# The z projection moved into the q, k, v stage of a hybrid decoder step

## The chip, the cores and the metric

The kernel runs on one core of a Trainium2 chip. The metric is the device time of one execution in microseconds (us). A profile is one such execution taken by the hardware profiler; its span runs from the first to the last instruction. Engines are named as in the profile: PE (matmul), PEld (its weight load), DVE, ACT, POOL, and SP, which here only issues transfers.

## The reference, cut to what matters

One layer works on 2048 new positions of one sequence (`x_prompt`) and on 8 x 8 sample tokens (`x_sample`), all in float32:

```
u = rmsnorm(h, norm_mix) @ w_in                       # 1024 -> q 512, k 256, v 256, z 512, xbc 1024, dt 8
q, k, v, z, xbc, dt = split(u)                        # rope on q, k
att = dilated window attention over q, k, v           # windows (128,1), (512,4), (2048,16), merged by their lse
xbc = silu(conv4(xbc));  y = chunked SSD(xbc, dt)     # Mamba-2, chunks of 128 positions
ssm = rmsnorm((y + d_skip * x) * silu(z)) * ssm_norm
h = h + concat(att, ssm) @ w_out
h = h + relu(rmsnorm(h) @ w_up)**2 @ w_down           # 1024 -> 4096 -> 1024
return rmsnorm(h), new k, v, conv and ssm states
```

The gate z is first needed by `silu(z)` of the SSD branch. Only the normalised input block and w_in's z columns are needed to compute it.

## The kernel before, in words

Every float32 product is taken as three matmuls of split operands: a tile is written as hi + lo, and `mm3` adds hi x hi, hi x lo and lo x hi in one PSUM bank. A split is one ACT copy and one DVE subtraction (`split`).

**First stage: q, k, v.** The 2048 positions are 8 blocks of 256 (`NB`, `BS`); the first two also carry 32 sample positions each (288 columns). `prep_x(i)` squares a block, sums it, takes the root (`rstd`, small matmuls `ps_r`), scales and splits it into four tiles `xq` (8 buffers, so two blocks stay on chip) and stores it to the scratch tensor `xn_s[i]`. Block i's turn is `qk_part` (6 groups of 24 matmuls, `ps_qk`, one per 128 rows of q and k) and `v_part` (2 or 3 position tiles of 24 matmuls, `ps_v`). In the middle of the turn, before group 2, stands `prep_x(i + 1)`. Groups are evicted by ACT and DVE into stage tiles `st`, which every second turn go out by 26 q stores and 16 k stores of 32 to 256 KB on SP's queue; k also goes out through a tile `kf` (2 buffers, `O["kT"]`), v through `vf` and its split differences `vhl` (1 buffer, `v3_s`). All PSUM tiles of the stage come from the pool `pa`, which has three of the eight banks.

**Second stage: attention.** 16 steps (4 key heads x 4 position blocks): `att_load` and `att_a` load k, q and v rows from scratch, take scores (`ps_qk` of line 573) and their maximum; `att_b` takes exponentials, splits them, multiplies with v (`ps_pv`) and sums (`ps_den`); `att_c` closes a head.

**Beside it: the other projections.** `g2(grp)` computes four 128-row groups of the z, x, B, C part over all 8 blocks (`ps_xz`, 24 matmuls for each group and block): it loads four weight tiles and then each block's four tiles `xq` again from `xn_s`, evicts with ACT (`ev`, line 797) and stores to `xz_s`. Its tiles lie in a pool `yp` that is open from the start of the program, so that its first loads lie in the first stage, held behind `k.gate`, the load of block 3. `g2(0)` and `g2(4)` are x, B and C; each block's first matmul is held behind an attention step (`k.steps`, two behind). `g2(8)` is z: it is written behind the attention, ahead of branch 0, held behind step 14, with four further buffers for its later blocks (`y8`).

**Third stage: branch 0, then the rest.** `branch(0)` does the SSD's first four chunks of 128 positions (`ssd`: convolution on DVE in line 904, transposes `ps_xt`, `ps_bt`, products `ps_y`, `ps_st`, `ps_yo`, the gated norm with `ps_ss`) and merges the attention outputs of the first 512 positions (`am<-o_s`). Then come output projection (`ps_o`) and MLP (`ps_up`, `ps_dn`) over four blocks of 512 positions, with the other branches in their shadow. The first `ps_o` matmul is held behind the last matmul that `mm3` issued (`k.zl`).

What sets the order: the kernel is written as above, and a scheduler places each engine's instructions in one fixed order, from the order of writing, the dependences and the holds named here. At run time each engine, and SP's queue, works in that order.

Of the kernel before, what the change touches and what calls it, by code (L numbers as in the profile page):

```python
# [110 lines left out]
def build(nc, tc, ctx, I, O, dbg=None, stop=None):  # L111
# [33 lines left out]
    yp = p1x.enter_context(tc.tile_pool(name="g2", bufs=1, reuse_waits="tile", side="right"))  # L145
# [7 lines left out]
    k.gate = None  # L153
# [17 lines left out]
    def load_w(src, pool=None, rp=None, after=None):  # L171
        rp = rp or yp
        if rp is yp:
            raw = yp.tile([P, 4 * NBX], F32, tag="xq", name="raw", bufs=XQ)[:, :D].rearrange("p (k m) -> p k m", k=KT)
        else:
            raw = gp.tile([P, KT, P], F32, tag=rp, name="raw")
        behind(nc.sync.dma_start(raw, src), k.gate if rp is yp else None)
        pl, nb = (pool, 2) if pool else (wp, GW)
# [38 lines left out]
    gp = g1x.enter_context(tc.tile_pool(name="g1", bufs=1))  # L217
# [6 lines left out]
    def load_x(i):  # L224
        n = nblk(i)
        xr_t[i] = []
        for q in range(2):
# [4 lines left out]
            xr_t[i] += [xr[:, 0:2, :n], xr[:, 2:4, :n]]
        if i == XG:
            k.gate = k.x
        tq_t[i] = gp.tile([P, 2, NBX], F32, tag="tq", name="tq", bufs=2)
        behind(nc.sync.dma_start(tq_t[i][:, :, :n], I["tabq"][i, :, :, :n]), k.x)

    def prep_x(i):
# [12 lines left out]
        rs = rstd(gp, ss, n, 1.0 / D)  # L251
# [9 lines left out]

    load_x(0)
# [16 lines left out]
    stage = {}
    v_t = {}  # L280
    for i in range(NB):
# [15 lines left out]
        def qk_part():  # L297
            for m in range(6):
                if m == 2 and i + 1 < NB:
# [8 lines left out]
                if m in (0, 4):  # L308
# [65 lines left out]
        def v_part():  # L374
# [3 lines left out]
            for (o, p0, mrows, c) in tiles:  # L378
                pv = slice(p0, p0 + mrows)
                ps = pa.tile([P, 512], F32, tag="pa", name="ps_v")[:mrows, :NV]  # L380
# [16 lines left out]
                vhl = gp.tile([P, 3, NKV, 2, HD], F32R, tag="vhl", name="vhl", bufs=1)  # L397
# [102 lines left out]
    g1x.close()  # L500
    if stop == "g1":
# [274 lines left out]
    def g2(grp, y8=None):  # L776
        ws = [load_w(I["wxz"][m]) for m in range(grp, grp + GR)]
        for i in range(NB):
            n = nblk(i)
            xn = []  # L780
            for q in range(4):
                pl, nb = (y8, Y8B) if y8 and i >= Y8 and q else (yp, XQ)
                xq = pl.tile([P, 4 * NBX], F32R, tag="xq", name="xq", bufs=nb)
# [3 lines left out]
            for m in range(grp, grp + GR):  # L787
# [4 lines left out]
                if m == grp and PACE and 2 * grp + i >= FST:  # L792
                    tc.add_manual_dep(f.ins, (k.steps[ZST] if grp == 8 else k.steps[max(0, 2 * grp + i - FST)]).ins.name,
# [4 lines left out]
                dq('z8' if grp == 8 else 'xz').dma_start(xz_s[m, :, i * BS:(i + 1) * BS], ev[:, :BS])  # L798
                if i < 2:
                    dq('z8' if grp == 8 else 'xz').dma_start(xzs_s[m, :, i * DS:(i + 1) * DS], ev[:, BS:])  # L800
# [276 lines left out]
    with tc.high_priority(offset=-G2LAG):  # L1077
        g2(8, p1x.enter_context(tc.tile_pool(name="y8", bufs=1, reuse_waits="tile", side="right")))
# [601 lines left out]
```

## Time and profile before

| | |
|---|---|
| median of 3 runs | 2765.54 us (2765.01 to 2772.32) |
| the profiled execution | 2767.76 us, span 2766.0 us |
| PE busy | 2617.2 us (95%) |
| DVE, ACT, POOL busy | 1710.1, 1161.3, 483.8 us |
| DMA | 481.62 MB, mean 174 GB/s |
| from 889 us to the end (output projection, MLP) | PE busy 1864.64 of 1877 us |

A row of busy time by stretch gives the stretch, its length, and each engine's busy time with its instruction count. A wait row gives who waited for whom, the sum, how often and the longest. A timeline row gives start, duration, engine, line, operation, output<-inputs, shapes, and in brackets the idle time before it and what ended it. A busy PE is a pipelined one: the spans of matmuls overlap, so a rate is a stretch divided by its count.

### The profile page before, as it was taken

Reading aid. Unit: us, or ns where it says so; the run is one execution under the profiler, and the core shown is the slowest. Engines: PE = TensorE matmul, PEld = TensorE weight load, DVE = VectorE, ACT = ScalarE, POOL = GpSimd, SP = SyncE. Lnnn points to the kernel's source line nnn. Section 1 sums busy time; section 2 is a strip of 40 time slices with the busy share of each in tenths; the row PEclk is TensorE's granted clock in tenths of the full one; section 3 lists DMA queues with packets and bytes.
Section 4 is the critical chain, followed back from the end, with each engine's and each line's share of the span. In section 5 each row is a group of like instructions: output and inputs, shape, how many; then the busy total and the mean of one; then the engine's idle time right before and its main releaser. Section 6 shows DMA issues by size and latency. Waiting matters only on the chain.

```text
span 2766.0 us, 42046 instructions
## 1 busy us (share of the span) xinstructions
PE 2617.2 (95%) x15190; PEld 2275.0 (82%) x15190; DVE 1710.1 (62%) x2995; ACT 1161.3 (42%) x2243; POOL 483.8 (17%) x406
## 2 busy tenths in 40 slices
PE   7979699999968999999999999999999999999998
PEld 7979688999857778888888886667688889999998
DVE  5545467777975646777567874445487764554555
ACT  5434245455643423444444442233254434332333
POOL 2222233544531200111210110020010003000000
PEclk9989899999988999999999999999999999999999
DMA  6887877786865745543574545456464534533332
GB/s 226 242 242 230 224 212 232 235 257 211 249 209 150 226 130 162 159 146 126 164 235 142 161 138 170 142 189 202 141 191 145 158 103 153 170 100 106 105 100 85
DMA packets 355265, 481.62 MB, mean 174 GB/s; under 512 B 38608, under 2 KB 230288, under 8 KB 354016
## 3 DMA queue, kind: packets, MB, share of 16 engines
q1 hardware_dynamic: 328592, 455.26, 53.3%
q10 hardware_dynamic: 26464, 23.66, 2.6%
q8 instruction: 120, 1.97, 0.3%
q14 instruction: 89, 0.73, 0.1%
HBM read 383.42 MB, written 128.96 MB: 185 GB/s over the span
## 4 chain that ended last, share of the span: by engine, by line
PE 80%; DMA 10%; DVE 4%; SPq 2%; issue 2%; POOL 1%; ACT 1%; ACTq 0%; DVEq 0%; POOLq 0%
PE ps_dn L1068 9%; PE ps_dn L1070 9%; PE ps_up L1070 9%; PE ps_up L1068 9%; PE ps_dn L1071 9%; PE ps_up L1071 9%; PE ps_qk L573 3%; PE ps_xz L186 2%; PE ps_xz L189 2%; PE ps_xz L190 2%; DMA xq<-xn_s 2%; PE ps_o L1070 2%; PE ps_o L1068 2%; PE ps_o L1071 2%; DMA xr<-xb 2%
## 5 line engine op out<-in xcount | busy, mean ns | idle before, releaser
L847 ACT ACTIVATE wm_h<-raw_m 128x512 fp32r<-128x512 f32 x576 | 362.3, 630 | 844.3 <-PE ps_dn L1070 484.2
L848 DVE TENSOR_TENSOR wm_l<-raw_m,wm_h 128x512 fp32r<-128x512 f32 x576 | 414.3, 721 | 116.7 <-ACT wm_h L847 104.4
L1068 PE MATMUL ps_dn<-uh,wm_h 128*128 128x512 f32 (+1 forms) x1280 | 458.5, 359 | 0.0
L1068 PE MATMUL ps_up<-xh_m,wm_h 128*128 128x512 f32 (+1 forms) x1280 | 458.4, 358 | 0.0
L1070 PE MATMUL ps_dn<-ul,wm_h 128*128 128x512 f32 (+1 forms) x1280 | 457.1, 357 | 0.0
L1070 PE MATMUL ps_up<-xl_m,wm_h 128*128 128x512 f32 (+1 forms) x1280 | 456.7, 357 | 0.0
L1071 PE MATMUL ps_dn<-uh,wm_l 128*128 128x512 f32 (+1 forms) x1280 | 456.0, 357 | 0.0
L1071 PE MATMUL ps_up<-xh_m,wm_l 128*128 128x512 f32 (+1 forms) x1280 | 455.8, 356 | 0.0
L1183 DVE TENSOR_TENSOR acc<-acc,ps_dn 128x512 f32<-128x512 f32 (+1 forms) x320 | 189.5, 593 | 242.4 <-PE ps_dn L1071 239.5
L1068 PEld LDWEIGHTS ps_dn<-uh,wm_h 128*128 128x128 f32 x1280 | 240.2, 188 | 43.5 <-issue 11.0
L1070 PEld LDWEIGHTS ps_dn<-ul,wm_h 128*128 128x128 f32 x1280 | 240.3, 188 | 39.0 <-issue 6.5
L1070 PEld LDWEIGHTS ps_up<-xl_m,wm_h 128*128 128x128 f32 x1280 | 241.0, 188 | 37.2 <-issue 4.5
L1071 PEld LDWEIGHTS ps_dn<-uh,wm_l 128*128 128x128 f32 x1280 | 240.5, 188 | 37.6 <-issue 4.1
L1071 PEld LDWEIGHTS ps_up<-xh_m,wm_l 128*128 128x128 f32 x1280 | 241.4, 189 | 35.5 <-issue 2.0
L1068 PEld LDWEIGHTS ps_up<-xh_m,wm_h 128*128 128x128 f32 x1280 | 241.2, 188 | 34.4 <-issue 0.8
L186 PE MATMUL ps_xz<-xq,wh 128*128 128x256 f32 (+1 forms) x768 | 224.2, 293 | 25.4 <-DMA xq<-xn_s 24.5
L189 PE MATMUL ps_xz<-xq,wh 128*128 128x256 f32 (+1 forms) x768 | 223.0, 291 | 0.0
L190 PE MATMUL ps_xz<-xq,wl 128*128 128x256 f32 (+1 forms) x768 | 221.9, 291 | 0.0
L1171 DVE SCALAR_TENSOR_TENSOR r<-ps_up,rs 128x512 f32<-128x512 f32 (+1 forms) x160 | 95.5, 597 | 141.1 <-PE ps_up L1071 140.3
L186 PEld LDWEIGHTS ps_xz<-xq,wh 128*128 128x128 f32 x768 | 149.9, 195 | 29.2 <-DMA xq<-xn_s 27.4
L1174 DVE TENSOR_TENSOR ul<-r,uh 128x512 fp32r<-128x512 f32 (+1 forms) x160 | 98.2, 614 | 92.6 <-ACT uh L1173 92.6
L189 PEld LDWEIGHTS ps_xz<-xq,wh 128*128 128x128 f32 x768 | 149.6, 195 | 1.0
(346 smaller groups left out, 4921.0 us busy)
## 6 DMA issues: line engine op xcount, KB each, us to landing
raw_m<-wup SPq DMA_DIRECT2D x256, 256.0 KB
raw_m<-wdn SPq DMA_DIRECT2D x256, 256.0 KB
xq<-xn_s SPq DMA_DIRECT2D x72, 512.0 KB
am<-o_s SPq DMA_DIRECT2D x128, 128.0 KB
raw_m<-wout SPq DMA_DIRECT2D x64, 256.0 KB
ks<-ck SPq DMA_DIRECT2D x32, 510.0 KB
vs<-cv SPq DMA_DIRECT2D x32, 510.0 KB
xq<-xn_s SPq DMA_DIRECT2D x24, 576.0 KB
```

Source lines behind the costliest of these rows:

```text
L186: r = nc.tensor.matmul(ps, wh(kk), xh(kk), start=kk == 0, stop=False)
L189: nc.tensor.matmul(ps, wh(kk), xl(kk), start=False, stop=False)
L190: k.zl = nc.tensor.matmul(ps, wl(kk), xh(kk), start=False, stop=kk == KT - 1)
L573: k.mm = nc.tensor.matmul(ov, kt[:, ksl], mv, start=first, stop=False, skip_group_check=True)
L847: k.at["ACT"] = nc.scalar.activation(hi, raw, AF.Copy)
L848: nc.vector.tensor_tensor(lo, raw, hi.bitcast(F32), op=ALU.subtract)
L1068: behind(nc.tensor.matmul(ps, wh[:, kk], xh(kk), start=first and kk == 0, stop=False), after)
L1070: nc.tensor.matmul(ps, wh[:, kk], xl(kk), start=False, stop=False)
L1071: r = nc.tensor.matmul(ps, wl[:, kk], xh(kk), start=False, stop=last and kk == nk - 1)
L1171: nc.vector.scalar_tensor_tensor(r, ps, 0.0, c(X.rs), op0=ALU.max, op1=ALU.mult)
L1174: nc.vector.tensor_tensor(c(ul), r, c(uh).bitcast(F32), op=ALU.subtract)
L1183: k.at["DVE"] = nc.vector.tensor_tensor(h, h, ps, op=ALU.add)
```

## The change

z (groups 8 to 11) is taken out of `g2` and computed in the first stage by a new function `z_part(i)`. It uses block i's `xq` tiles while they are still on chip. `z_part(i - 1)` stands at the head of turn i, and `z_part(7)` behind the last turn. Its four weight tiles are loaded into `xq` buffers that are free at the start (`rawz`) and split once, before group 2 of turn 0. Its evictions go to the tag `kf` (2 buffers, shared with the k stores) and out to `xz_s` on SP's queue.

Beside that: a pool `px1` of five PSUM banks in the first stage (3 for `ps_v` and `ps_z`, 2 for the norm), so that all eight are in use there and `pa`'s three are left to q and k; `vhl` has 2 buffers; the rotation table `tq` has 1 buffer and is loaded behind group 4 of the turn before; the pool `yp` opens behind the first stage, so that the first loads of `g2(0)` follow it; and `y8`, the hold at step 14 and the re-read of `xn_s` for z are gone. The sum of the matmuls is the same. With `g2(8)` gone, `k.zl` names the last matmul of `g2(4)`.

```diff
-    yp = p1x.enter_context(tc.tile_pool(name="g2", bufs=1, reuse_waits="tile", side="right"))
...
-    gp = g1x.enter_context(tc.tile_pool(name="g1", bufs=1))
+    gp = g1x.enter_context(tc.tile_pool(name="g1", bufs=1, reuse_waits="tile"))
+    px1 = g1x.enter_context(tc.tile_pool(name="px1", bufs=1, space=PSUM, reuse_waits="tile"))
...
-        tq_t[i] = gp.tile([P, 2, NBX], F32, tag="tq", name="tq", bufs=2)
-        behind(nc.sync.dma_start(tq_t[i][:, :, :n], I["tabq"][i, :, :, :n]), k.x)
+
+    def load_tq(i):
+        n = nblk(i)
+        tq_t[i] = gp.tile([P, 2, NBX], F32, tag="tq", name="tq", bufs=1)
+        nc.sync.dma_start(tq_t[i][:, :, :n], I["tabq"][i, :, :, :n])
...
-        rs = rstd(gp, ss, n, 1.0 / D)
+        rs = rstd(gp, ss, n, 1.0 / D, None, px1.tile([P, 512], F32, tag="r", name="ps_r", bufs=2))
...
+    rawz = [gp.tile([P, 4 * NBX], F32, tag="xq", name="rawz", bufs=8)[:, :D].rearrange("p (k m) -> p k m", k=KT)
+            for _ in range(4)]
...
+    for m in range(4):
+        nc.sync.dma_start(rawz[m], I["wxz"][8 + m])
+    wz = []
...
+                if m == 2 and i == 0:
+                    for r in range(4):
+                        wz.append(load_w(None, gp, None, k.px, rawz[r]))
...
-                ps = pa.tile([P, 512], F32, tag="pa", name="ps_v")[:mrows, :NV]
+                ps = px1.tile([P, 512], F32, tag="v", name="ps_v", bufs=3)[:mrows, :NV]
...
-                vhl = gp.tile([P, 3, NKV, 2, HD], F32R, tag="vhl", name="vhl", bufs=1)
+                vhl = gp.tile([P, 3, NKV, 2, HD], F32R, tag="vhl", name="vhl", bufs=2)
...
+        def z_part(i):
+            n, xn = nblk(i), xn_t.pop(i)
+            for m in range(4):
+                wh, wl = wz[m]
+                ps = px1.tile([P, 512], F32, tag="v", name="ps_z", bufs=3)[:, :n]
+                mm3(ps, lambda kk: wh[:, kk], lambda kk: wl[:, kk], lambda kk: xn[kk // 2][:, 0, kk % 2],
+                    lambda kk: xn[kk // 2][:, 1, kk % 2], n)
+                ev = gp.tile([P, NBX], F32, tag="kf", name="ev", bufs=2)[:, :n]
+                nc.scalar.activation(ev, ps, AF.Copy)
+                dq('xz').dma_start(xz_s[8 + m, :, i * BS:(i + 1) * BS], ev[:, :BS])
+                if i < 2:
+                    dq('xz').dma_start(xzs_s[8 + m, :, i * DS:(i + 1) * DS], ev[:, BS:])
+
+        if i:
+            z_part(i - 1)
         for part in ((v_part, qk_part) if i == NB - 1 else (qk_part, v_part)):
             part()
+    z_part(NB - 1)
...
     g1x.close()
+    yp = p1x.enter_context(tc.tile_pool(name="g2", bufs=1, reuse_waits="tile", side="right"))
...
-    with tc.high_priority(offset=-G2LAG):
-        g2(8, p1x.enter_context(tc.tile_pool(name="y8", bufs=1, reuse_waits="tile", side="right")))
```

What the scheduler makes of it is seen at three places. First ACT's order from the v tiles of turn 2 into turn 3, before and in the change (`sq` belongs to the norm of a block to come, `sw` is the first read of turn 3's group 0):

```order
L388 ACTIVATE vf<-ps_v 128x264
L245 ACTIVATE sq<-xr 128x2x256
L388 ACTIVATE vf<-ps_v 128x264
L245 ACTIVATE sq<-xr 128x2x256 x2
L310 ACTIVATE sw<-ps_qk 64x256
L311 ACTIVATE sw<-ps_qk 64x256
```

```order
L398 ACTIVATE vf<-ps_v 128x264
L244 ACTIVATE sq<-xr 128x2x256
L103 ACTIVATE vhl<-vf 128x4x64
L244 ACTIVATE sq<-xr 128x2x256
L103 ACTIVATE vhl<-dv 128x4x64 x2
L426 ACTIVATE ev<-ps_z 128x256 x4
L318 ACTIVATE sw<-ps_qk 64x256
L319 ACTIVATE sw<-ps_qk 64x256
```

The four z evictions now stand between the v splits of one turn and the first read of the next.

Second SP's order at the change of stage, from the last k stores to the attention's first loads, before and in the change (the two `xz_s` stores before are of x/B/C group 0, the four of the change are of z):

```order
L372 DMA k_s_82<-st_2396 32x1024 x4
L798 DMA xz_s<-ev 128x256
L800 DMA xzs_s<-ev 128x32
L798 DMA xz_s<-ev 128x256
L518 DMA m_3105<-m 128x256
L521 DMA mf<-m 128x512 x2
L563 DMA kA<-k_s_81 64x2x512
```

```order
L382 DMA k_s_82<-st_2986 32x1024 x4
L427 DMA xz_s<-ev 128x256 x4
L545 DMA m_4037<-m 128x256
L548 DMA mf<-m 128x512 x2
L590 DMA kA<-k_s_81 64x2x512
```

All four stores of the last z part stand ahead of the attention's loads. The weights and the first block of `g2(0)`, which before were loaded ahead of this place, now follow the attention's loads:

```order
L752 DMA V_4886<-v_s 128x16x128
L171 DMA raw<-wxz 128x1024 x4
L811 DMA xq<-xn_s_70 128x1152 x4
L811 DMA xq<-xn_s_71 128x1152 x2
L593 DMA qt<-q_s_79 64x2x512 x4
```

Third PE's order in branch 0, behind the first chunk's products, before and in the change:

```order
L941 MATMUL ps_y<-ar,xdt 64x128 x4
L955 MATMUL ps_st<-xw,bt 128x256 x2
L941 MATMUL ps_y<-ar,xdt 64x128 x4
L186 MATMUL ps_xz<-xq,wh 128x256
L189 MATMUL ps_xz<-xq,wh 128x256
```

```order
L967 MATMUL ps_y<-ar,xdt 64x128 x4
L981 MATMUL ps_st<-xw,bt 128x256 x2
L967 MATMUL ps_y<-ar,xdt 64x128 x4
L1003 MATMUL ps_ss<-ones_r,sq_9389 128x1 x2
L947 MATMUL ps_xt<-ident,cv 128x128 x4
L955 MATMUL ps_bt<-ident,cv 128x128
```

Between these chunks before stand 18 z matmuls, whose first waits for a block of `xn_s`. In the change the next chunk's matmuls follow at once, and the first three matmuls of the output projection come a few rows behind them.

More of the change, by code (lines that the diff above doesn't have):

```diff
@@ L38 @@
 GW = 4
-G2LAG = 0
+XG = 3
 PACE = True
-Y8 = 4
-Y8B = 4
-ZST = 14
 FST = 2
 NBC = 2
-XG = 3
 HB = 4
@@ L151, in behind @@
         return d
-    k.gate = None
     k.at = {}
@@ L169, in build, with load_w @@
     pn.tensor = nc.tensor
[L171 to L178, printed above, removed]
+    def load_w(src, pool=None, rp=None, after=None, raw=None):
+        if raw is None:
+            if rp is None:
+                raw = yp.tile([P, 4 * NBX], F32, tag="xq", name="raw", bufs=XQ)[:, :D].rearrange("p (k m) -> p k m", k=KT)
+            else:
+                raw = gp.tile([P, KT, P], F32, tag=rp, name="raw")
+            nc.sync.dma_start(raw, src)
+        pl, nb = (pool, 6) if pool else (wp, GW)
         hi = pl.tile([P, KT, P], F32R, tag="wh", name="wh", bufs=nb)
@@ L267, in build @@
     wq.append(load_w(I["wqk"][1], None, "st1", k.px))
+    load_tq(0)
     load_x(1)
@@ L314, in qk_part @@
                     nc.vector.tensor_tensor(sw, sw, tq[:, 1, :n], op=ALU.mult)
+                if m == 4 and i + 1 < NB:
+                    load_tq(i + 1)
                 if m < 4:
@@ L773, in build, with g2 @@
         G_, T = Gn, Tn
-    def g2(grp, y8=None):
+    def g2(grp):
         ws = [load_w(I["wxz"][m]) for m in range(grp, grp + GR)]
@@ L781, in g2 @@
             for q in range(4):
-                pl, nb = (y8, Y8B) if y8 and i >= Y8 and q else (yp, XQ)
-                xq = pl.tile([P, 4 * NBX], F32R, tag="xq", name="xq", bufs=nb)
+                xq = yp.tile([P, 4 * NBX], F32R, tag="xq", name="xq", bufs=XQ)
                 xq = xq.rearrange("p (j k n) -> p j k n", j=2, k=2)[:, :, :, :n]
@@ L792, in g2 @@
                 if m == grp and PACE and 2 * grp + i >= FST:
-                    tc.add_manual_dep(f.ins, (k.steps[ZST] if grp == 8 else k.steps[max(0, 2 * grp + i - FST)]).ins.name,
+                    tc.add_manual_dep(f.ins, k.steps[2 * grp + i - FST].ins.name,
                                       mybir.DependencyInfo(mybir.DependencyClass.NoSync, mybir.DependencyReason.DATA),
@@ L797, in g2 @@
                 nc.scalar.activation(ev, ps, AF.Copy)
-                dq('z8' if grp == 8 else 'xz').dma_start(xz_s[m, :, i * BS:(i + 1) * BS], ev[:, :BS])
+                dq('xz').dma_start(xz_s[m, :, i * BS:(i + 1) * BS], ev[:, :BS])
                 if i < 2:
-                    dq('z8' if grp == 8 else 'xz').dma_start(xzs_s[m, :, i * DS:(i + 1) * DS], ev[:, BS:])
+                    dq('xz').dma_start(xzs_s[m, :, i * DS:(i + 1) * DS], ev[:, BS:])
     for grp in (0, 4):
```

## The prediction

> **What bounds the kernel now.** I read the table of busy time by stretch first. Its columns are the stretch, its length, then PE, PEld, DVE, ACT and POOL busy with instruction counts, the granted clock, the DMA engines' busy share and GB/s. The cuts are where the roles change: turns 2 to 5 of the q, k, v stage, turns 6 and 7, the change of stage, the attention up to the last matmul of the x/B/C groups, the attention's end, and branch 0 until the output projection starts. Behind it stand the four last of these stretches again with the instructions of `ps_xz` alone.
>
> ```profile
> core 0: us, PE busy (x) PEld busy (x) DVE busy (x) ACT busy (x) POOL busy (x), PEclk, DMA share, GB/s
> 86.75:116.40 29.65, 26.68 (x201) 26.46 (x202) 16.35 (x35) 12.31 (x30) 8.86 (x13) 0.89 0.75 212
> 116.40:155.00 38.60, 26.42 (x202) 26.02 (x202) 15.50 (x37) 12.43 (x30) 8.57 (x12) 0.82 0.87 270
> 155.00:184.00 29.00, 25.83 (x202) 25.40 (x201) 16.56 (x34) 14.54 (x34) 12.49 (x16) 0.94 0.83 258
> 184.00:213.40 29.40, 25.89 (x203) 25.54 (x203) 15.18 (x37) 11.99 (x30) 6.98 (x9) 0.94 0.78 236
> 213.40:262.00 48.60, 47.28 (x394) 46.86 (x392) 32.92 (x75) 24.20 (x57) 13.40 (x15) 1.00 0.71 232
> 262.00:305.00 43.00, 15.12 (x108) 14.30 (x108) 4.14 (x15) 4.34 (x16) 0.00 (x0) 0.76 0.91 211
> 305.00:672.00 367.00, 344.94 (x2419) 337.54 (x2420) 268.39 (x324) 177.61 (x324) 162.45 (x105) 0.95 0.77 226
> 672.00:781.00 109.00, 96.32 (x657) 91.19 (x656) 97.54 (x139) 69.93 (x140) 54.44 (x33) 0.91 0.78 242
> 781.00:889.00 108.00, 76.94 (x570) 71.14 (x571) 68.88 (x145) 41.91 (x96) 22.27 (x21) 0.85 0.60 178
> ...
> 305.00:672.00 367.00, 204.55 (x1415) 190.54 (x1415) 22.79 (x59) 0.95 0.77 226
> 672.00:781.00 109.00, 62.37 (x427) 58.12 (x427) 6.73 (x18) 0.91 0.78 242
> 781.00:889.00 108.00, 51.16 (x366) 48.07 (x366) 6.00 (x16) 0.85 0.60 178
> ```
>
> The q, k, v stage is PE's: in turns 6 and 7 it is busy 47.28 of 48.60 us, DVE 32.92. So is the attention up to 672 us (344.94 of 367). From there it is different: to 781 us DVE is the fullest engine (97.54 of 109), and z, which is all of `ps_xz` there, holds PE for 62.37 us beside it; to 889 us no engine is full, and z holds PE for 51.16 us. z is work of PE that now lies where PE is not the bound.
>
> In the q, k, v stage PE's idle time has one main cause. The first row is PE's waits from 16 to 262 us, the second ACT's in turn 3 (us in total, times, longest); the others are SP's sequencer there.
>
> ```profile
> PE ps_v L384 <- ACT kf L345: 21.0, 5, 11.9
> ACT vhl L107 <- issue: 13.1, 1, 13.1
> 121.77 2.49 SPq L177 DMA_DIRECT2D raw<-wxz  x4
> 126.14 0.67 SPq L405 DMA_DIRECT2D v_s<-vhl  x1
> 129.98 17.82 SPq L338 DMA_DIRECT2D q_s<-st  x18
> ```
>
> The second v tile of a turn waits for one of three banks that the k eviction still holds. In turn 3 ACT stands 13.1 us at a `vhl` split, whose single buffer waits for the v store of 126.14 us; that store is queued behind early loads of the next stage (`raw<-wxz` at 121.77 us), and the q stores slow to a microsecond each.
>
> **The change, part by part.** The pace first, `ps_qk` alone and then z's form with 288 columns:
>
> ```profile
> 244.60:261.90 17.30, 17.27 (x144) 17.06 (x144) 2.08 (x5) 2.75 (x8) 1.00 0.61 210
> 266.00:279.20 13.20, 13.06 (x96) 12.82 (x96) 0.82 (x2) 1.00 0.69 155
> ```
>
> That is 17.27 / 144 = 0.120 us and 13.06 / 96 = 0.136 us a matmul.
>
> *1. z in the stage.* Seven z parts stand at the heads of turns 1 to 7: 2 x 96 matmuls x 0.136 + 5 x 96 x 0.120 = 26.1 + 57.6 = **+83.7 us**. The eighth (11.5 us) stands behind the last q, k part. The 32 evictions on ACT and the four weight splits are in no sum: PE is the bound, and in turns 2 to 5 ACT has at most 14.54 us of work in 29, DVE 16.56.
>
> *2. Stalls that go.* Turns 2 to 5 last 29.65 + 38.60 + 29.00 + 29.40 = 126.65 us; at the pace above their 192 matmuls each would take 4 x 23.04 = 92.2, and the few norm matmuls some 4 us by what the stretch of turns 6 and 7 has over (48.60 - 46.1 = 2.5 for one norm and two turns). So 30.5 us are lost there to waits and to the low clock behind them. The change takes away each cause: v and z have three banks of their own, the norm two; `vhl` has two buffers; the early loads of the next stage are gone; and the norm of the block after has z's 11.5 us more. New is that z's evictions share the two `kf` buffers with the k stores on SP's queue. Bounds: 34 us (these and what turn 1 and the first turn lose), and 10 us (turn 3's 13.1 alone, less 3 for new waits). I take **-28**, near the upper end, since each cause has its remedy.
>
> *3. The change of stage.* These are PE's wait there and SP's issues:
>
> ```profile
> PE ps_qk L573 <- DMA V<-v_s: 25.9, 1, 25.9
> 271.88 1.29 SPq L366 DMA_DIRECT2D k_s<-st  x4
> 279.38 0.38 SPq L798 DMA_DIRECT2D xz_s<-ev  x1
> 282.29 0.57 SPq L563 DMA_DIRECT2D kA<-k_s  x1
> 296.27 0.39 SPq L595 DMA_DIRECT2D V<-v_s  x1
> ```
>
> SP issues q and k stores until 279 us, 17 us behind the last q, k matmul, then the attention's loads; PE runs 13.06 us of x/B/C meanwhile and waits 25.9. In the change z(7) fills the same place with 11.5 us, and its four stores stand ahead of the loads where two stood; z(7) ends before SP is through the k stores, so the loads start about when they do now. **0**, between -5 (no x/B/C loads beside them) and +7 (four stores wait for z).
>
> *4. The attention up to the end of the x/B/C groups.* Their first block, 96 matmuls, is no longer done at the change of stage: +13.1 us in a stretch that PE fills to 94%. Their weights and first block are now loaded behind the attention's own loads, so PE finds no filler for its first waits: +3, an estimate between nothing and the 9 us that they would be if the two loads (512 x 4 + 576 x 4 KB, 4.4 MB at 226 GB/s, 20 us) hit those waits in half of their time. **+16**, between 5 (most falls into PE's 22 idle us) and 22.
>
> *5. 672 to 781 us.* 62.37 us of PE go, but DVE's 97.54 of 109 stay: at most 11.5. **-7** (0 to -11.5).
>
> *6. 781 to 889 us.* First PE's wait for z's blocks and SP's wait for z's evictions (672 to 889 us), then the end of the chain on DVE.
>
> ```profile
> PE ps_xz L186 <- DMA xq<-xn_s: 17.1, 5, 12.8
> SPq L798 <- ACT ev L797: 45.6, 15, 11.3
> 854.28 1.95 DVE L967 SCALAR_TENSOR_TENSOR y<-cv,dskip,y 128x128 f32<-128x128 f32 x4
> 861.51 0.16 DVE L978 TENSOR_SCALAR rc_s<-ps_ss 128x2 f32<-128x2 f32 x1 [5.29 <-PE ps_ss L977]
> 862.01 0.69 DVE L925 TENSOR_TENSOR xdt<-ps_xt,dtv 128x512 f32<-128x512 f32 x1 [0.34 <-PE ps_xt L921]
> 872.85 1.14 DVE L967 SCALAR_TENSOR_TENSOR y<-cv,dskip,y 128x128 f32<-128x128 f32 x4
> 880.06 0.16 DVE L978 TENSOR_SCALAR rc_s<-ps_ss 128x2 f32<-128x2 f32 x1 [6.08 <-PE ps_ss L977]
> 884.74 1.12 DVE L985 SCALAR_TENSOR_TENSOR y<-y,normw,ps_ss 128x128 f32<-128x128 f32 x4 [4.52 <-PE ps_ss L982]
> 886.67 0.69 DVE L108 TENSOR_TENSOR mix<-y,mix 128x512 fp32r<-128x512 f32 x1 [0.81 <-ACT mix L107]
> ```
>
> Branch 0's matmuls stand behind z's on PE, and z's behind its loads. From the first `y` (854.28) to the last `mix` (886.67) DVE stands idle for most of 33 us. The last chunk's `xdt` of 862.01 could follow the `y` that ends at 856.23, were its transposes not behind z on PE: some 6 us, and 4 more for its next matmuls. The two waits for `ps_ss` behind the last `y` (6.08 and 4.52 us) hold POOL and ACT work and z; I take half, 5. Together 15 us. Another 8 come from the earlier chunks' share of the 17.1, and 3 because the output projection no longer has to follow z's last matmul. **-26**, between -15 and -39 (108 - 68.88, DVE's floor).
>
> The sum is 83.7 - 28 + 0 + 16 - 7 - 26 = **+38.7 us** on an execution of 2767.76 (span 2766.0). The median shown is 2.2 below it, so I put the sum on the median: 2765.5 + 38.7 = **2804 us**. All lower ends: 83.7 - 34 - 5 + 5 - 11.5 - 39 = -1, all upper: 83.7 - 10 + 7 + 22 - 0 - 15 = +88.
>
> [...]
>
> **The rivals.** *A: the late stretch doesn't shorten.* It is a chain over DVE, ACT, POOL and DMA, and z only fills its holes; without z PE stands still there and its clock is low, as in this row, where a matmul behind a wait takes 0.41 us and not 0.28:
>
> ```profile
> 806.24 0.58 PE L186 MATMUL ps_xz<-xq,wh 128*128 128x256 f32 x1 [12.80 <-DMA xq<-xn_s]
> 806.62 0.41 PE L189 MATMUL ps_xz<-xq,wh 128*128 128x256 f32 x1
> ```
>
> Time: 2765.5 + 83.7 - 28 + 16 = 2837. For it: DVE's 97.54. Against: the waits of part 6.
>
> *B: the stage packs and the late stretch falls to DVE's floor.* Parts 2, 5 and 6 at their ends: 83.7 - 34 + 16 - 11.5 - 39 = +15, so 2781. Against: DVE work there hangs on loads and evictions too.
>
> *C, the other side: bytes set the pace.* z's re-read of the block is gone:
>
> ```profile
> xq<-xn_s SPq DMA_DIRECT2D x72, 512.0 KB
> xq<-xn_s SPq DMA_DIRECT2D x24, 576.0 KB
> ```
>
> A third of it, 24 x 512 + 8 x 576 KB, is 17.3 MB, 73 us at the 242 and 226 GB/s of the stretches. If DMA (0.78 of it busy) and not DVE holds the late stretch, it ends up to 73 us earlier; and with DMA at 0.75 to 0.91 before it, parts 2 to 4 come out at their lower ends, since z's work then fits beside transfers. 83.7 - 34 - 5 + 5 - 73 = -23, so 2742. It decides from the point where parts 2, 3, 5 and 6 give over 100 us together. Against: in 781 to 889 us, where z waits longest, DMA is at 0.60.
>
> That the change does something else than it says is no rival: the order of instructions has z where the text has it.
>
> **How the numbers follow.** Forecast (2785 to 2825) 0.55, A 0.17, B 0.15, C 0.13. The measurement tells 0.3%, 8 us, from no change. Slower: the forecast, A and B, 0.87, less 0.10 for the tails of the forecast and B near nought: 0.77. Faster: C but for 0.01, 0.12. The rest, 0.11, is the same. Range: 2766 to 2838, from B's lower side to A; C is left out. The forecast's own is 2785 to 2825.
>
> **What would show it.** In the profile after: last q, k matmul near 262 + 83.7 - 28 = 318 us, no `ps_v` wait over 3 us there (step 2); some 43 us from it to the attention's first matmul (3); the last `ps_xz` near 744 (4: 672 + 55.7 + 16); the first full output matmuls near 928 (889 + 38.7), DVE full to the attention's end (5) and PE mostly idle in both (6). The forecast is wrong if ACT's z evictions wait for stores by tens of us (slower), or if the attention's end comes before 781 + 20 us (faster).

## The result and the profile after

The changed kernel takes 2805.4 us (median of 4 runs, 2802.5 to 2807.4) against 2765.9 us for the kernel before, run beside it: a ratio of 1.0137, with a 95% interval of 1.0119 to 1.0155. It is 1.4% slower. The prediction said 2804 us.

The profiled execution took 2806.49 us, its span is 2804.8 us. Its busy time by stretch, cut at the same events as before (the whole q, k, v stage as one row):

```profile
core 0: us, PE busy (x) PEld busy (x) DVE busy (x) ACT busy (x) POOL busy (x), PEclk, DMA share, GB/s
16.00:314.50 298.50, 288.36 (x2318) 285.32 (x2318) 139.66 (x299) 119.82 (x285) 67.10 (x81) 0.99 0.64 201
314.50:355.00 40.50, 13.27 (x108) 12.45 (x106) 2.59 (x8) 3.78 (x15) 0.00 (x0) 0.69 0.87 193
355.00:736.00 381.00, 358.39 (x2567) 353.04 (x2567) 280.99 (x335) 188.64 (x341) 162.41 (x105) 0.97 0.78 227
736.00:834.00 98.00, 54.67 (x203) 42.40 (x203) 94.17 (x130) 57.00 (x110) 52.67 (x33) 0.60 0.45 127
834.00:928.50 94.50, 43.77 (x213) 31.94 (x211) 65.37 (x140) 36.09 (x80) 25.88 (x21) 0.64 0.41 126
928.50:2805.00 1876.50, 1865.61 (x9774) 1546.07 (x9774) 1129.09 (x2064) 749.14 (x1403) 175.41 (x157) 0.99 0.46 150
```

The stage is PE's more than ever (288.36 us busy of 298.50). The two stretches from 736 to 928.5 us are 11 and 13.5 us shorter than their counterparts. PE is busy there for only 54.67 of 98 and 43.77 of 94.5 us, and its clock fell from 0.91 and 0.85 to 0.60 and 0.64. From 928.5 us on nothing changed (1876.5 us against 1877).

To compare many kernels I use four events of each trace, read from the rows of PE's matmuls by tile. The numbers behind `x384` and the like are the least, median and longest duration in ns, then the first and the last start in us. First before, then the changed kernel:

```profile
L190 PE MATMUL ps_qk<-xq,wl x384: 274/283/445, 18.9 to 261.6; 128*128 128x256 f32 x144, 128*128 128x288 f32 x48
L573 PE MATMUL ps_qk<-qt,kA x300: 272/386/602, 305.1 to 723.3; 128*128 128x256 f32 x150
L718 PE MATMUL ps_den<-dh,ones_r x32: 388/394/764, 356.6 to 780.2; 128*128 128x512 f32 x32
L1068 PE MATMUL ps_up<-xh_m,wm_h x1280: 288/392/774, 940.8 to 2726.8; 128*128 128x512 f32 x110, 128*128 128x288 f32 x73
```

```profile
L184 PE MATMUL ps_qk<-xq,wl x384: 276/280/561, 18.5 to 314.2; 128*128 128x256 f32 x144, 128*128 128x288 f32 x48
L600 PE MATMUL ps_qk<-qt,kA x300: 272/386/606, 355.1 to 780.0; 128*128 128x256 f32 x150
L745 PE MATMUL ps_den<-dh,ones_r x32: 387/396/796, 406.1 to 833.0; 128*128 128x512 f32 x32
L1094 PE MATMUL ps_up<-xh_m,wm_h x1280: 288/392/774, 979.4 to 2765.9; 128*128 128x512 f32 x110, 128*128 128x288 f32 x73
```

They cut the span in five. "Stage" runs to the last q, k matmul, "change" from there to the attention's first matmul, "attention" to the start of its last `ps_den<-dh`, "late" to the MLP's first `ps_up`, and "rest" to the end. In us:

| | stage | change | attention | late | rest | span |
|---|---|---|---|---|---|---|
| before | 261.6 | 43.5 | 475.1 | 160.6 | 1825.2 | 2766.0 |
| changed | 314.2 | 40.9 | 477.9 | 146.4 | 1825.4 | 2804.8 |
| difference | +52.6 | -2.6 | +2.8 | -14.2 | +0.2 | +38.8 |

So z cost 52.6 us net where it went and freed 14.2 us where it came from. PE's waits in the stage (16 to 314.5 us; total, times, longest):

```profile
PE ps_r L206 <- ACT dg L205: 7.3, 3, 2.8
PE ps_qk L180 <- ACT xq L103: 1.7, 1, 1.7
PE ps_qk L183 <- DVE xq L104: 1.4, 1, 1.4
PE ps_z L180 <- ACT vf L398: 1.4, 3, 0.6
```

And one of ACT's there:

```profile
ACT ev L426 <- DMA xz_s<-ev: 15.3, 5, 5.9
```

The 21.0 us for `ps_v` are gone. ACT does wait for z's stores, as the prediction feared, but PE's three waits in front of `ps_z` come to 1.4 us together. In branch 0 (834 to 929 us) PE's largest waits are these:

```profile
PE ps_ss L1003 <- POOL sq L998: 23.4, 4, 12.7
PE ps_o L1094 <- ACT mix L103: 13.5, 3, 9.4
PE ps_o L1096 <- DVE mix L104: 7.3, 3, 3.3
```

One of them in the timeline:

```profile
889.38 0.79 PE L1094 MATMUL ps_o<-mix,wm_h 128*128 128x512 f32 x1 [9.39 <-ACT mix L103]
```

PE no longer waits for z's blocks. It waits in front of the chunks' norm matmuls, and in front of output matmuls that now stand among the chunks' own, since `k.zl` names an earlier matmul.

### The profile page after: what moved, and what is told of

Same layout as the page of the kernel before. It is cut to its first block, busy times and chain, and to the rows that moved or that the text cites. A ratio compares the mean times of both kernels' runs of the same rounds, so it can differ in the third digit from the quotient of the medians.

```text
span 2804.8 us, 41924 instructions
## 1 busy us (share of the span) xinstructions
PE 2627.4 (94%) x15190; PEld 2274.1 (81%) x15190; DVE 1718.9 (61%) x2995; ACT 1164.7 (42%) x2243; POOL 487.3 (17%) x406
## 3 DMA queue, kind: packets, MB, share of 16 engines
q8 instruction: 120, 1.97, 0.3%
## 4 chain that ended last, share of the span: by engine, by line
PE 84%; DMA 6%; DVE 5%; SPq 2%; issue 2%; ACT 1%; POOL 1%; DVEq 0%; ACTq 0%; POOLq 0%
PE ps_dn L1094 9%; PE ps_dn L1096 9%; PE ps_up L1096 9%; PE ps_up L1094 9%; PE ps_dn L1097 9%; PE ps_up L1097 9%; PE ps_qk L600 3%; PE ps_o L1096 2%; PE ps_o L1094 2%; PE ps_o L1097 2%; PE ps_xz L180 2%; PE ps_xz L183 2%; PE ps_xz L184 2%; PE ps_po L1531 1%; PE ps_pv L724 1%
## 5 line engine op out<-in xcount | busy, mean ns | idle before, releaser
L1094 PEld LDWEIGHTS ps_dn<-uh,wm_h 128*128 128x128 f32 x1280 | 240.3, 188 | 43.5 <-issue 11.0
L180 PE MATMUL ps_xz<-xq,wh 128*128 128x256 f32 (+1 forms) x512 | 146.6, 288 | 7.2 <-DMA xq<-xn_s 7.1
L183 PE MATMUL ps_xz<-xq,wh 128*128 128x256 f32 (+1 forms) x512 | 146.6, 287 | 0.0
L184 PE MATMUL ps_xz<-xq,wl 128*128 128x256 f32 (+1 forms) x512 | 145.8, 286 | 0.0
L600 PE MATMUL ps_qk<-qt,kA 128*128 128x256 f32 x300 | 103.5, 355 | 41.1 <-DMA qt<-q_s 35.1
L1196 ACT ACTIVATE r<-r 128x512 f32<-128x512 f32 (+1 forms) x160 | 88.8, 555 | 115.4 <-DVE r L1195 114.6
```

Source lines behind the costliest of these rows:

```text
L180: r = nc.tensor.matmul(ps, wh(kk), xh(kk), start=kk == 0, stop=False)
L183: nc.tensor.matmul(ps, wh(kk), xl(kk), start=False, stop=False)
L184: k.zl = nc.tensor.matmul(ps, wl(kk), xh(kk), start=False, stop=kk == KT - 1)
L600: k.mm = nc.tensor.matmul(ov, kt[:, ksl], mv, start=first, stop=False, skip_group_check=True)
L1094: behind(nc.tensor.matmul(ps, wh[:, kk], xh(kk), start=first and kk == 0, stop=False), after)
```

## The experiments

The kernel before was timed again beside each group of runs, at medians of 2771.0 to 2772.8 us, against 2765.9 us beside the changed kernel, so I compare ratios with their intervals. A difference of two ratios can still be 5 to 7 us off, since before's time moved between the groups and the changed kernel's need not have. How far a trace's cut can be trusted is seen from stages of unchanged code: three profiled executions of before's stage end at 261.6, 265.9 and 265.5 us, five of the changed one's between 312.8 and 315.8 us. Against before, a stage is therefore known to some 4 us.

**1. Before without z.**

```diff
-    with tc.high_priority(offset=-G2LAG):
-        g2(8, p1x.enter_context(tc.tile_pool(name="y8", ...)))
-            nc.sync.dma_start(L.zt, xz_s[8:12]...)
+            nc.sync.dma_start(L.zt, xz_s[0:4]...)
```

> The kernel before with the z group g2(8) left out whole: its 32 loads of the block, 4 of weights, 768 matmuls, evictions and stores. The gate reads x rows in z's place, so the output is not the reference's. This is the price of z in its old place. Forecast's theory (z fills a late stretch that DVE and chains bound): parts 5 and 6 as forecast, 2766 - 7 - 26 = 2733; by what the changed kernel's trace shows of these two stretches (-11 and -13), 2742. Rival A (the late stretch does not shorten): 2766. Rival C (bytes set the pace): 2766 - 73 = 2693.

Measured: 2756.9 us, ratio 0.9950 (0.9935 to 0.9965). All of z, 768 matmuls with its loads and stores, cost 14 us in its old place. On the expectations' scale (before at 2766) that is 2752: 19 and 10 us over the forecast's two figures, 14 under rival A's and 59 over rival C's, so none of them is met: it lies between the second figure and A. Attention 473.6 us, late 148.0:

```profile
L718 PE MATMUL ps_den<-dh,ones_r x32: 387/396/792, 361.9 to 784.5; 128*128 128x512 f32 x32
L1068 PE MATMUL ps_up<-xh_m,wm_h x1280: 288/392/774, 932.5 to 2719.0; 128*128 128x512 f32 x110, 128*128 128x288 f32 x73
```

The late part falls by 12.6 us, the attention by 1.5. The x/B/C groups' last matmul starts at 685.6 us here. From it to the attention's end it is 100 us and not 109, but the stretch ahead of it is 374.7 us and not 367: z among the attention's matmuls cost next to nothing. As in the changed kernel, `k.zl` here names an earlier matmul and output matmuls stand among the chunks' own, the first at 814.8 us; run 8 asks what that costs.

**2. The changed kernel without z.**

```diff
-        if i:
-            z_part(i - 1)
...
-    z_part(NB - 1)
```

(and z's rows replaced as above)

> The changed kernel with its eight z parts left out (768 matmuls, 32 evictions and their stores; z's weights are still loaded and split). The gate reads x rows in z's place, so the output is not the reference's. This is the price of z in the q, k, v stage. Forecast's theory (PE is the bound there and z pays its full pace): 83.7 of the seven parts go and part of the eighth's 11.5, so 2805 - 84 to - 95 = 2710 to 2721. Rival (z hides the waits of the stage, which come back when it is gone): the stage saves only 50 to 60, 2745 to 2755.

Measured: 2723.1 us, ratio 0.9822 (0.9803 to 0.9841), 87 us below the changed kernel's 1.0137 by ratio. The theory holds in the time by ratio; the spans of the two profiled executions differ by 80.5 us (2804.8 and 2724.3). Its last q, k matmul and PE's largest wait in the stage:

```profile
L184 PE MATMUL ps_qk<-xq,wl x384: 276/281/561, 18.7 to 242.0; 128*128 128x256 f32 x144, 128*128 128x288 f32 x48
```

```profile
PE ps_r L195 <- POOL ss L249: 14.1, 4, 4.4
```

The stage ends 72.2 us earlier, not 83.7, since waits come back that z lay over: the norm's sums on POOL hold PE for 14.1 us. The attention is 6.5 us shorter, the late part 1.9.

**3. to 6. Stage remedies without moving z.** Each is the kernel before with one or both of

```diff
+    px1 = g1x.enter_context(tc.tile_pool(name="px1", bufs=1, space=PSUM, reuse_waits="tile"))
-        rs = rstd(gp, ss, n, 1.0 / D)
+        rs = rstd(gp, ss, n, 1.0 / D, None, px1.tile([P, 512], F32, tag="r", name="ps_r", bufs=2))
-                ps = pa.tile([P, 512], F32, tag="pa", name="ps_v")[:mrows, :NV]
+                ps = px1.tile([P, 512], F32, tag="v", name="ps_v", bufs=3)[:mrows, :NV]
```

```diff
-                vhl = gp.tile([P, 3, NKV, 2, HD], F32R, tag="vhl", name="vhl", bufs=1)
+                vhl = gp.tile([P, 3, NKV, 2, HD], F32R, tag="vhl", name="vhl", bufs=2)
```

Both edits:

> The kernel before with z in its old place and two of the change's other parts alone: five PSUM banks of their own in the stage (three for v, two for the norm), and two buffers for vhl. The early loads of the next stage stay. Forecast's theory (step 2: the stalls of the stage come from the banks and from vhl, not from missing work): 2766 - 28 = 2738, at least 2766 - 20. Rival (in the changed kernel the 31 us of stalls went because z's matmuls lie over them, or because the early loads are gone): 2760 or more.

The banks alone:

> The kernel before with the five PSUM banks of their own in the stage alone (three for v, two for the norm); vhl keeps its one buffer. With both edits the stage's last q, k matmul came at 250.8 us and not 261.6, 10.8 earlier, and the time fell by 0.6%. Theory of the banks (PE's wait for ps_v, 21.0 us in five waits, is what they remove): 8 to 11 us earlier, time 0.3 to 0.6% under before. Theory of vhl (turn 3's ACT wait of 13.1 us is the root and the ps_v wait its consequence): under 4 us, time within 0.15% of before.

`vhl` alone:

> The kernel before with two buffers for vhl alone; v and the norm keep sharing the three banks with q and k. Theory of the banks: the turn with the 13.1 us wait gets shorter by some 5 and others not at all, because the k eviction still holds the bank; last q, k matmul at 256 to 261 us, time within 0.2% of before. Theory of vhl: 8 to 11 us earlier, 0.3 to 0.4% under before.

Both edits, and the gate of the early loads moved (`XG = 3` to `XG = 7`):

> The kernel before with banks, two vhl buffers and, in addition, the next stage's early loads held back until the last block of x is loaded (gate at block 7 instead of 3). z stays in its old place. Theory (the stage of the changed kernel without z ends at 242.0 us and that of before with banks and vhl at 250.8; the 8.8 us between are stores queued behind these loads): last q, k matmul at 242 to 245 us, time 0.9% under before, and the x/B/C matmuls at the change of stage start later without moving the attention's first matmul. Rival (the 8.8 us come from elsewhere, or the loads only move into the q and k stores of the last turns): 249 us or later, no better than 0.6% under before.

| | time, us | ratio (95%) | stage | change | attention | late |
|---|---|---|---|---|---|---|
| 3: both | 2754.6 | 0.9943 (0.9928 to 0.9958) | 250.8 | 44.5 | 472.6 | 159.4 |
| 4: banks | 2754.9 | 0.9942 (0.9925 to 0.9958) | 249.6 | 45.0 | 472.7 | 160.7 |
| 5: vhl | 2763.5 | 0.9976 (0.9964 to 0.9988) | 264.7 | 40.1 | 478.9 | 156.0 |
| 6: both, loads later | 2752.9 | 0.9939 (0.9924 to 0.9953) | 246.9 | 45.8 | 475.6 | 160.8 |

PE's largest waits in the stage, first with the banks alone (no `ps_v` among them), then with `vhl` alone:

```profile
PE ps_r L201 <- POOL ss L251: 9.6, 4, 4.5
PE ps_qk L186 <- ACT kf L346: 8.8, 1, 8.8
```

```profile
PE ps_v L384 <- ACT kf L345: 17.8, 4, 10.6
PE ps_r L201 <- POOL ss L250: 11.6, 4, 4.2
```

The banks do all of it: 16 us in time, and 12 in the stage against the profile of before shown above, 16 against the two later ones. With two `vhl` buffers and the old banks PE still waits 17.8 us for `ps_v`, and the stage ends no earlier (264.7 us, against 256 to 261 expected). This kernel is nevertheless 7 us faster (0.12 to 0.36%, where the theory of the banks had at most 0.2); its trace has 3.4 us less in the change and 4.6 less late, and I have no cause for either. Both edits together are no better than the banks, 16 us by ratio, less than the 20 that the theory gave at least and more than the rival's 6: about half or more of the 31 us that the changed kernel's stage recovers is something else. Holding back the early loads gains 4 us in the stage, between the theory's 242 to 245 us and the rival's 249, and nothing that the times can tell (0.9939 against 0.9943). The 8.8 us were not theirs alone.

Why two `vhl` buffers did not help is seen in ACT's and PE's rows of turn 3, first in before, then in run 5. ACTq is ACT's own queue of transfers, here the stores of the normalised block:

```profile
143.37 3.02 ACTq L259 DMA_DIRECT2D xn_s<-xq  x3
146.43 0.42 ACT L107 ACTIVATE vhl<-vf 128x256 fp32r<-128x256 f32 x1 [13.08 <-issue]
149.20 0.77 ACT L345 ACTIVATE kf<-ps_qk 32x256 f32<-32x256 f32 x2 [1.74 <-DMA q_s<-st]
150.02 0.59 PE L384 MATMUL ps_v<-wvh,xq 128*128 128x264 f32 x1 [11.86 <-ACT kf L345]
```

```profile
144.24 5.77 ACTq L259 DMA_DIRECT2D xn_s<-xq  x4
150.12 0.76 ACT L345 ACTIVATE kf<-ps_qk 32x256 f32<-32x256 f32 x2 [14.72 <-DMA xn_s<-xq]
150.93 0.59 PE L384 MATMUL ps_v<-wvh,xq 128*128 128x264 f32 x1 [10.63 <-ACT kf L345]
```

In both ACT stands still until it issues these stores, and its next operation follows them: in before the `vhl` split, in run 5 the k eviction. So the wait was not the `vhl` buffer's. And PE did wait for it: its longest wait of the stage ends at the k eviction behind it. What the first store waited for is open.

All four are faster than both kernels. The banks alone, three changed lines, end 16 us under before and 54 under the changed kernel by ratio.

**7. All of the change but z.** The changed kernel without its z parts, with `g2(8)` of before written back behind the attention.

```diff
-        if i:
-            z_part(i - 1)
...
+    with tc.high_priority(offset=-G2LAG):
+        g2(8, p1x.enter_context(tc.tile_pool(name="y8", ...)))
```

> All that the change does beside z, with z back in its old place: the changed kernel without its z parts and z's weights in the stage, and with the z group g2(8) of before behind the attention, its pace and its own buffers. So five PSUM banks in the stage, two vhl buffers, no early loads of the next stage, block 0 of x/B/C in the attention. Theory by sums of the runs so far (stage without z to 242 us, change of stage 41, attention 472 to 479, from its last den to the first up matmul 159 to 160, the rest 1826): 2740 to 2748, 0.9% under before, and below the kernel with banks and vhl alone (0.6%). Rival (without the early loads z's and x/B/C's groups come later and the attention or branch 0 grows): 0.5% under before or less.

Measured: 2758.0 us, ratio 0.9954 (0.9941 to 0.9966): no better than the banks alone, so the rival's time and not the theory's. Attention 475.7 and late 158.7 us are as the theory had them. The stage and the change are not: the stage ends at 255.3 us and not at 242, and the change takes 45.1 us and not 41. One premise also fell: without z's weights in the stage's buffers the pool of the second stage had room, and its first weights were loaded at 8 us and not behind the stage. Two waits hold PE, and ACT's largest wait is of a like length:

```profile
PE ps_qk L184 <- DVE t L317: 19.6, 2, 10.4
```

```profile
ACT st L107 <- DMA xn_s<-xq: 31.9, 3, 12.4
```

One of the three in ACT's rows:

```profile
136.51 5.57 ACTq L262 DMA_DIRECT2D xn_s<-xq  x4
142.18 0.73 ACT L107 ACTIVATE st<-kf 128x256 fp32r<-128x256 f32 x2 [11.52 <-DMA xn_s<-xq]
```

Each of the three ends as in turn 3 of before: right behind stores of the normalised block that ACT issues itself, here four. In run 2 the three longest waits at these splits came to 4.9, 4.6 and 3.0 us. Why the stores were issued later here is open.

With run 2 this kernel gives a second price of z in its old place: 2758.0 less 2723.1 is 35 us, and not run 1's 14. The late part has 14.2 of it, near run 1's 12.6; but 13.3 lie in the stage and 4.3 in the change, where no z matmul stands. So what z costs late agrees. The rest is open: the two kernels also differ in z's weights and in the early loads.

**8. Output matmuls out of the way.**

```diff
-        nc.tensor.matmul(pr_[:, :256], ones, f1(dg), start=True, stop=True, skip_group_check=True)
+        k.zl = nc.tensor.matmul(pr_[:, :256], ones, f1(dg), start=True, stop=True, skip_group_check=True)
```

> The changed kernel with the output projection's first matmul put behind branch 0's last matmul instead of behind the x/B/C groups' last, so that its first twelve matmuls do not stand between the chunks' matmuls. Theory (PE takes its work in order, and the chunks' matmuls wait behind output matmuls that wait for mix; this is where 13 of part 6's forecast 26 us went): 2805 - 10 = 2795. Rival (the chunks' chain over DVE, POOL and ACT at PE's low clock sets the end, the early output matmuls cost nothing): 2805, or up to 3 slower since twelve matmuls come later.

Measured: 2801.2 us, ratio 1.0103 (1.0086 to 1.0120), against 1.0137 (1.0119 to 1.0155): the intervals touch. The difference is 9 us by ratio, 4.2 us by the two medians, and 3.0 us in the spans, 1.5 of it late and the rest in cuts that the edit doesn't reach. PE's 20.8 us of waits in front of `ps_o` were mostly waits that the chunks' own matmuls then had: those in front of `ps_ss` behind POOL's `sq` grow from 23.4 to 40.8 us. The late part, where the theory's 10 us had to show, bears out the rival, and the ratio taken alone would bear out the theory; the times do not settle it.

What held the chunks then? The stretch between the norm matmuls of chunk 0 and chunk 1, first here, then in before; the second row of each has the convolution taps on DVE alone:

```profile
857.50:888.30 30.80, 10.13 (x44) 7.89 (x44) 30.03 (x68) 13.55 (x34) 10.94 (x7) 0.56 0.53 161
857.50:888.30 30.80, 12.61 (x38) 0.56 0.53 161
```

```profile
810.00:835.30 25.30, 16.81 (x143) 15.92 (x141) 21.19 (x40) 10.92 (x25) 8.33 (x7) 0.97 0.74 217
810.00:835.30 25.30, 5.17 (x11) 0.97 0.74 217
```

DVE is busy 30.03 of 30.80 us: 38 of branch 0's 96 convolution taps lie in it, 11 in before.

**9. and 10. Fewer convolution taps.** The same edit in the changed kernel (with the output matmuls held as in 8) and in before:

```diff
-            for tap in range(3):
+            for tap in range(3 if nb == 1 else 1):
```

> The changed kernel with the output projection behind branch 0's last matmul, and in branch 0 alone two of the three convolution taps on DVE left out (64 operations of 0.3 us or more; the output is not the reference's). In the run with that order and all taps DVE was busy 30.0 of the 30.8 us between the norm matmuls of chunk 0 and chunk 1, with 38 taps in it, 12.6 us; 10 taps, 4.9 us, stand in that stretch of before. Theory (with z gone DVE is the bound of that stretch, which is why branch 0 gave 13 us and not 26): that stretch 6 to 9 us shorter, first output matmul 82 to 85 us behind the attention's last den matmul instead of 90.4. Rival (the chain over loads, POOL and PE at its low clock holds it, and DVE only fills it): 88 us or more.

> The kernel before with the same two taps left out in branch 0 (the output is not the reference's); z in its old place. Theory (with z there PE's queue and z's loads hold the chunks, and DVE has room): first output matmul 104 us or more behind the attention's last den matmul, 107.5 in before. Rival (DVE bounds both kernels alike): as much earlier as in the changed kernel, 98 to 101 us.

| | time, us | ratio (95%) | attention | late |
|---|---|---|---|---|
| changed, held (8) | 2801.2 | 1.0103 (1.0086 to 1.0120) | 476.7 | 144.9 |
| the same, fewer taps | 2792.5 | 1.0068 (1.0051 to 1.0084) | 470.8 | 140.4 |
| before | | 1 | 475.1 | 160.6 |
| before, fewer taps | 2766.3 | 0.9980 (0.9970 to 0.9990) | 474.9 | 158.9 |

In the changed kernel the stretch between the two norm matmuls falls from 30.8 to 24.3 us, and DVE is no longer full in it:

```profile
851.50:875.80 24.30, 9.12 (x44) 7.32 (x44) 19.90 (x35) 12.74 (x34) 7.82 (x7) 0.57 0.53 158
```

That is within the theory's 6 to 9 us. The first output matmul comes 86.1 us behind the last den matmul, between the theory's 85 and the rival's 88: 0.7 and 1.4 us are given back ahead of this stretch and behind it. The attention's end gains 5.9 us more, which I had not expected to see there; the same cut lies between 471.4 and 478.9 us in the other kernels, so this gain can't be put down to the taps. In before the same 64 operations less give 0.2 us in the attention and 1.7 late; its first output matmul stands 104.4 us behind the last den matmul, as the theory had it, and the turn of chunk 1 does not shorten (norm to norm 25.2 us, and 29.2 without the taps). So DVE binds that turn in the changed kernel and not in before, where z shared PE's queue with the chunks. For the whole stretch the pair does not show as much: the first output matmul comes 4.3 us earlier in the changed kernel and 3.1 in before, and the time falls by 0.35% and by 0.20%.

**11. and 12. Useless matmuls meant to hold the clock.** Behind each chunk's state matmuls, in the kernel of 8:

```diff
+        if nb > 1:
+            pw = psd("ps_w")
+            for _ in range(60 if c < 3 else 30):
+                k.mm = behind(nc.tensor.matmul(pw[:, :P], ones_r, ones_r, ...), k.mm)
```

and the next norm matmul behind them; in the second run 100, 115, 55 and 40.

> The changed kernel with the output projection behind branch 0's last matmul, as in the run that held it, and with 210 useless 128x128 matmuls on constants in branch 0: 60 behind the state matmuls of each of the first three chunks and 30 in the last, in front of the next norm matmul, at a place where PE waited 5 to 15 us. They compute nothing that is used. Theory of the clock (TensorE's granted clock of 0.65 there doubles the chunk's small matmuls, some 4 us a chunk on the chain, and z's matmuls kept it up in the kernel before): branch 0's chunks shorten, first output matmul 6 to 12 us earlier than the 922.4 of that run. Rival (PE is off the chain there; DVE, POOL and the loads set it): within 2 us of it, or later by the useless matmuls that the norm matmul now waits for.

> As the run with 210 useless matmuls, but with 100, 115, 55 and 40 of them behind the four chunks' state matmuls, so that at 0.117 us each they last until the norm matmul's input is there. In that run the clock was 1.00 while they ran and 0.50 again at the norm matmuls 2 to 10 us later, so that it didn't test the clock. They compute nothing that is used. Theory of the clock: the norm, transpose and B matmuls behind them run at 0.13 to 0.14 us and not 0.25, and the first output matmul comes 4 to 10 us earlier than 90.4 us behind the attention's last den matmul. Rival (DVE's, POOL's and the loads' chain sets the end): the small matmuls are faster, but the first output matmul stays within 2 us of 90 us behind the last den, or comes later.

Measured: 2812.4 us, 1.0152 (1.0136 to 1.0168), and 2817.5 us, 1.0166 (1.0150 to 1.0181): slower, with the first output matmul 94.5 and 102.9 us behind the last den matmul. The first did not test the clock in three of the four chunks, since it fell in the gaps behind the useless matmuls: it was 1.00 over them and 0.50, 0.50 and 0.52 over the chunks' small matmuls, behind gaps of 9.6, 5.6 and 2.1 us (the section on the hardware has the rows of the last). The second did in part: behind the norms of chunks 1 and 2 the norm, transpose and B matmuls ran at 0.14 to 0.16 us (in run 8 at 0.23, 14 of them in 3.25 us at a clock of 0.50), and from norm to norm it then took 17.1 and 12.1 us, against 17.4 and 13.2 in run 8. With the clock up there these two turns were 0.3 and 1.1 us shorter. The added matmuls also changed the order that the scheduler gave DVE and POOL: in the second run PE waited 16.4 us for a scale of chunk 0's norm, whose first step stood on DVE behind convolution taps and a merge that waited for its load. As a test of the clock over the whole branch the pair is inconclusive.

## Why the prediction was right, and where its steps were not

The time was right to 1.4 us, and the sum (+38.7) met the span's difference (+38.8). That the sum was so close is luck: step by step the measured values lie off by -3.1 us (the stage), -2.6 (the change), -6.2 (the attention) and +11.8 (branch 0), which cancel.

- **Step 1 and 2, the stage: +83.7 - 28 = +55.7 forecast, +52.6 measured.** Right in size. The pace of 0.120 us held (the stage is PE's, 288.36 of 298.50 us), so 31.1 us of stalls went, within the bounds. "The change takes away each cause" is where the reasoning was only partly right. Of the causes named, the banks are worth 12 to 16 us (run 4) and `vhl` none in the stage (run 5). Turn 3's 13.1 us on ACT were read wrongly: ACT stood there in front of its own stores of the normalised block, and with two `vhl` buffers it still stood 14.7 us. Some 11 us are no stall removed but a stall covered, 83.7 less the 72.2 that the stage got shorter by without z (run 2); the argument on the norm, which was to have z's 11.5 us more, was of this kind. The 4 to 8 us left are not settled: the early loads account for some 4 (run 6), no more than the stage of before varies by, and putting all the other edits together without z gave 255.3 us, not 242 (run 7).
- **Step 3, the change of stage: 0 forecast, -2.6 measured.** Right within its bounds.
- **Steps 4 and 5, the attention: +16 - 7 = +9 forecast, +2.8 measured.** By their own cuts they came out at +13.7 (305 to 672 is now 355 to 735.8) and -11 (109 us is now 98), close to both. But the cut was no wall. The attention as a whole takes 471 to 479 us in all fourteen kernels, with block 0 in it or not, with z in it or not. PE's matmuls are filler there up to the end, and the 13.1 us of block 0 were not a cost to add but a shift of the line between filler and none. I read PE's 344.94 of 367 us as its bound, but filler takes what time it finds, and a full PE that holds much of it is no bound. What does bind the attention as a whole no run here shows.
- **Step 6, branch 0: -26 forecast, -13 measured, -14.2 to the MLP's first matmul.** This is the term that was mis-sized. The mechanism was there: z's waits left PE's queue and the chunks moved up. From the last chunk's chain I took 15 us, and from chunk 2's norm to the full output matmuls it went from 27.3 us (861.0 to 888.3) to 19 (909.5 to 928.5), so 8. Of the earlier chunks' 8 came 4. "3 because the output projection no longer has to follow z's last matmul" came to nothing: it now stood among the chunks, though that cost only 1.5 (run 8). So each of the three terms was too large, and even the smaller bound of 15 was not reached. One reason is shown: I set the other bound by DVE's 68.88 us of 108, as if that work were spread evenly, and asked of no chunk whether DVE has room in it. With z gone, 12.6 us of convolution lie in chunk 1's turn, DVE is full there, and taking two taps away shortens that turn by 6.5 us (run 9). Why the last chunk gave 8 us and not 15 no run shows.
- **The rivals.** *A* (2837) was nearer than I thought in one respect: z's 113.5 us of PE work from 672 to 889 us (62.37 + 51.16) cost 14 us in its old place, by run 1. It fails by those 14 us and by the attention, where block 0 cost 2.8 and not 16. So nearly nine tenths of that work (99.5 us) cost nothing where it stood, and the whole change cost 38.8 us. *B* (2781) had the late stretch fall to DVE's sum of busy time, which it did not reach: DVE is busy 65.37 of 94.5 us there now. *C* (2742) is refuted: with the 17.3 MB gone and DMA down to 0.41 to 0.45 in the two late stretches, they gave 24 us and not 73, and with z gone altogether from before (run 1) the time fell by 14.

The stage's gaps repeated: five `ps_v` waits for the k eviction, one in each of five turns, 21.0 us in all. In run 4 none of them is left, and five banks instead of a share of three took 12 us out of the stage.

## What to carry to other kernels

Before work is moved out of a stretch, measure the stretch without it: z's price was not its 113.5 us of PE time but the 14 us that its removal gave there (35 in a kernel with the other edits), and in the stage where PE is full it paid 72 to 87 us. When a change brings remedies of its own along, try these without the move: five banks alone were faster than either kernel. And in a stretch with several engines near their limits, look for the densest turn of the next engine rather than its mean.

## What the runs showed of the hardware

**The clock was down behind a gap of 2.1 us.** These are stretches of run 11: 60 useless matmuls, the 2.1 us behind them in which PE did nothing, and the chunk's small matmuls that follow.

```profile
905.60:912.60 7.00, 6.97 (x62) 6.80 (x60) 6.29 (x11) 1.16 (x2) 1.68 (x2) 1.00 0.16 39
912.60:914.70 2.10, 0.00 (x0) 0.00 (x0) 0.00 (x0) 0.63 (x1) 1.35 (x2) 1.00 0.00 0
914.70:918.00 3.30, 3.25 (x15) 3.25 (x16) 1.45 (x3) 0.74 (x3) 0.70 (x1) 0.52 0.04 7
```

The granted clock is 1.00 over 7 us of dense work and over the gap of 2.1 us, and 0.52 over the 3.3 us behind the gap. In before, z's first 18 matmuls behind a wait of 12.80 us ran for 3.8 us at 0.54 and the next ones at 1.00. The length of the gap alone does not tell the clock: in before PE did nothing from 828.5 to 835.25 us, and the clock was 1.00 over the first 4.0 us of this gap, 0.70 over the next 2.8 and 0.50 over the 4.7 us behind them. What sets the point of the fall no run here shows.

**Four DVE operations and a POOL sum took longer beside the other engine's work.** Four DVE operations and three POOL operations of chunk 1, first in the kernel of run 8, then the same four and the last POOL sum in before:

```profile
877.06 3.10 DVE L993 SCALAR_TENSOR_TENSOR y<-cv,dskip,y 128x128 f32<-128x128 f32 x4
877.34 1.07 POOL L985 TENSOR_TENSOR hst<-hst,cdec 128x512 f32<-128x512 f32 x1
878.74 1.26 POOL L1043 TENSOR_TENSOR am<-am 128x512 f32<-128x512 f32 x1 [0.33 <-DMA am<-o_s]
884.55 3.71 POOL L998 TENSOR_TENSOR sq<-sq 128x256 f32<-128x256 f32 x1 [2.68 <-ACT sq L997]
```

```profile
826.66 1.13 DVE L967 SCALAR_TENSOR_TENSOR y<-cv,dskip,y 128x128 f32<-128x128 f32 x4
833.92 1.28 POOL L972 TENSOR_TENSOR sq<-sq 128x256 f32<-128x256 f32 x1 [0.27 <-ACT sq L971]
```

The four take 3.10 us where two POOL operations run beside them and 1.13 where POOL is idle. The POOL sum takes 3.71 us beside a dense run of convolution taps, and 1.28 in before, where DVE was busy for all of the 1.28 us too, but only 0.62 of it with a tap. In the three other chunks it takes 0.73 to 0.75 us in before and 0.72 to 0.75 in the changed kernel; in before DVE was idle beside two of these and busy with taps for all of the third, of 0.75 us. The two long ones stand on the chain of the packed chunk and are 4.4 us of it (1.97 + 2.43). So not every overlap went with a longer time, and why these did no run here separated.
